# Seven block products for the q, k, z and gate projections, and attention by query block with the output projections as its fill

## The chip, the core and the metric

The kernel runs on one core of a Trainium2 chip. The metric is the device time of one execution in microseconds (us), the median of several runs. Five engines work beside each other, each through its own queue in order: TensorE (PE; matmuls, PEld is its weight load), VectorE (DVE), ScalarE (ACT), GpSimd (POOL) and SyncE (SP), which here only issues DMAs. Matmul results land in PSUM, here in tiles (banks) of up to 128 x 512 floats; the other tiles lie in SBUF. F32R is a rounded float format.

## The reference

One layer on x of 2048 tokens by 1024 channels, all in float32:

- h = RMSNorm(x); one projection of h to 8720 columns: z gate and x, B, C, dt of the SSD branch, q, k, v and z gate of attention, and 2 x 1024 branch gates.
- SSD branch: causal convolution over four tokens, SiLU, softplus of dt, a chunked scan over 16 heads of 64 channels and 128 states; then SiLU gate and group RMSNorm; y_ssd = y @ w_ssd_proj.
- Attention branch, 16 heads of 64 channels: for each query the logits q.k / 8 of the earlier keys; w = sigmoid(logit) times the product of sigmoid(-logit') over all keys between that key and the query; o = w @ v; y_sb = (o * SiLU(z_sb)) @ w_sb_proj.
- merged = sigmoid(gates) weighted sum of y_ssd and y_sb; out = x + RMSNorm(merged @ w_out).

## The kernel before

Tokens are taken in four blocks (tb) of 512. A value that goes into a projection is split into a high and a low F32R part (`split`, lines 680 to 682: a cast on ACT, a subtraction on DVE, both 128 x 512), and each product is three matmuls, high by high, high by low, low by high. A projection tile is 128 output columns by 512 tokens: eight slices of 128 input channels, so 24 matmuls (`product`, `proj`), with the weights split by `prep_w` (line 134) into two halves of 128 x 512.

The work runs in four stages.

1. Input: x is normalized, transposed on PE and kept in SBUF as hh and hl for all four blocks. Then q/k columns 0, 1, 8 and 9 (column 0 also holds dt), 16 tiles in all, and the v columns, which put tokens on partitions (`unit_v`).
2. SSD: per group B and C, then per pair of heads a z and an x column, with convolution on DVE, scan states and outputs in between; the first z column of attention at the end. Results go to `ytd` in DRAM.
3. Attention: 160 steps of (head, query block, key block), head by head; 64 of them on the diagonal. `attn_qk` (lines 827 to 858) makes for each of the four rows i of 128 queries the logits (two matmuls), two sigmoids on ACT, t = sigmoid(-logit) (line 840) and w = sigmoid(logit) (line 842), on the diagonal two masking selects on POOL (844, 846), the running product of t along the keys as a scan on DVE (849), the gating multiply w * t on DVE (850), and a copy of the carry for the next step on POOL (853). `attn_tr` transposes w on PE and ACT copies it to SBUF (870); `attn_av` multiplies with v, and at the end of a head and block o is summed and gated on DVE (890, 891). Between these pieces `fill` hands out projection matmuls at an even rate: the other 34 columns of q, k, z and gates (3264 matmuls) and, in the last head, the y projection of one block (192).
4. Output, block by block: y is normalized (sums of squares by `y_load`, line 693, `y_norm` with the product at 719), y and o are projected, gated, merged, and multiplied by w_out; then the norm and the residual.

The order on PE is the order of the program text, held by `chain`; the other engines are put in order by a scheduler that goes by program order and readiness. `later(n, fn)` issues work n matmuls later. The loop of stage 3:

```
for s in range(len(steps)):
    attn_load(s + 2)
    for i in range(CPB):
        attn_tr(s, i)
        attn_qk(s + 1, i)
        fill(i)
        if i == 1 and s > 0:
            attn_av(s - 1)
            fill(CPB)
```

Of the kernel before, what the change touches and what calls it, by code (L numbers as in the profile page):

```python
# [48 lines left out]
def hybrid_kernel(ctx, tc, x, norm_pre, w_in, b_gate, conv_w, conv_b, dt_bias, a_log, d_skip,  # L49
# [61 lines left out]
    csd = drp.tile([HEADS, L], F32, name="csd")  # L111
    ytd = [drp.tile([D, TB], F32, name=f"ytd{t}") for t in range(NTB)]
# [4 lines left out]
    hp, close_hp = opened(name="hp", bufs=8)  # L117

    def big(dtype, name):
        return hp.tile([P, KT, TB], dtype, name=name, tag="h", bufs=8)  # L120

    hh, hl = [], []
    KH = KT // 2

    def prep_w(pool, bufs, src, col0, eng=None):
        hi, lo = [], []
        for half in range(2):
            raw = pool.tile([P, KH, P], F32, name="wraw", tag="wraw", bufs=2)
            nc.sync.dma_start(
                raw, src[half * KH * P:(half + 1) * KH * P, col0:col0 + P].rearrange("(k p) c -> p k c", p=P))  # L130
            h = pool.tile([P, KH, P], F32R, name="whi", tag="whi", bufs=bufs)
            nc.scalar.copy(h, raw)  # L132
            l = pool.tile([P, KH, P], F32R, name="wlo", tag="wlo", bufs=bufs)
            (eng or nc.vector).tensor_tensor(l, raw, h.bitcast(F32), op=ALU.subtract)  # L134
            hi.append(h)
            lo.append(l)
        return hi, lo
# [23 lines left out]

    def run(gen):
        for _ in gen:
            clock[0] += 1
            while events and events[0][0] <= clock[0]:
                heapq.heappop(events)[2]()
# [53 lines left out]
    ev, close_ev = opened(name="ev", bufs=2)  # L220

    with tc.tile_pool(name="p0", bufs=2) as p0, tc.tile_pool(name="p0p", bufs=1, space=PSUM) as p0p:
        def load_x(tb):
            ts = []
            for c in range(CPB):
                xt = p0.tile([P, D], F32, name="xt", tag="xt", bufs=8)
                nc.sync.dma_start(xt, x[(tb * CPB + c) * P:(tb * CPB + c + 1) * P, :])
                ts.append(xt)
            return ts
# [33 lines left out]
        def normalize(xs, first=False):  # L263
            for c0 in range(0, CPB, 2):
# [7 lines left out]
                if first and c0 == 0:  # L272
                    lead_in.append(i)
# [791 lines left out]
```

## Time and profile before

| | |
|---|---|
| time, median of 3 runs | 3059.14 us (3056.71 to 3060.24) |
| profiled execution: its time, its span | 3057.36 us, 3055.6 us |
| PE busy, instructions | 3012.0 us (99%), 16169 |
| DVE busy | 2140.1 us (70%), 3653 |
| ACT busy | 1585.5 us (52%), 3102 |
| POOL busy | 505.3 us (17%), 1690 |
| granted TensorE clock, mean | 0.995 |
| moved by DMA | 303.84 MB, 99 GB/s |

The span is from the first to the last instruction. Matmuls are pipelined: the busy time of one (0.4 us) is longer than the distance from one to the next, so the pace is read from a long stretch. A busy time counts what an instruction waits for once it has started, also a wait for another engine's access. The chain that ended last is PE for 88%, with the projections alone for 49%.

### The profile page before, as it was taken

The page shows a single profiled execution, that of the slowest core. Times are in us where ns is not written, and L with a number is a line of the kernel's source. Part 1 is how long each engine was busy: PE and PEld are TensorE (multiplying, and loading weights), DVE is VectorE, ACT ScalarE, POOL GpSimd, SP SyncE. Part 2 cuts the span into 40 slices and gives each one's busy share as a digit, 9 for nine tenths or more (in the row PEclk, how much of TensorE's full clock was granted, in tenths as well). Part 3 has the DMA queues.
Part 4 walks back from the last instruction along what each step waited for, and adds up shares of the span by engine and source line. Part 5 has one row for each costly group of instructions (what it writes and reads, how often), then busy time and mean ns, then how long its engine had stood idle before and what let it go on. Part 6 is the DMA issues. An engine that isn't in the chain of part 4 may idle for free.

```text
span 3055.6 us, 47953 instructions
## 1 busy us (share of the span) xinstructions
PE 3012.0 (99%) x16169; PEld 2342.6 (77%) x16169; DVE 2140.1 (70%) x3653; ACT 1585.5 (52%) x3102; POOL 505.3 (17%) x1690
## 2 busy tenths in 40 slices
PE   8999999999999999999999999999999999999998
PEld 6899888788887777777777777777777667888887
DVE  7310578868877777878778878877777798756653
ACT  6221345534546666666666666666666565333321
POOL 0000001001101222222222221222122331101000
PEclk9999999999999999999999999999999999999999
DMA  5522122202233333324323333334233345545452
GB/s 166 142 72 52 28 58 77 78 25 76 81 90 109 101 86 94 93 85 108 94 77 101 97 86 96 89 90 118 66 87 92 114 136 158 178 131 179 131 165 70
DMA packets 298812, 303.84 MB, mean 99 GB/s; under 512 B 55916, under 2 KB 196040, under 8 KB 298568
## 3 DMA queue, kind: packets, MB, share of 16 engines
q1 hardware_dynamic: 298416, 300.73, 34.3%
q8 instruction: 130, 2.13, 0.3%
q14 instruction: 114, 0.93, 0.1%
q10 hardware_dynamic: 152, 0.05, 0.0%
HBM read 208.28 MB, written 92.41 MB: 98 GB/s over the span
## 4 chain that ended last, share of the span: by engine, by line
PE 88%; DVE 7%; DMA 3%; issue 1%; ACT 0%; POOL 0%; SPq 0%; ACTq 0%; DVEq 0%; POOLq 0%
PE proj L74 49%; PE po L74 14%; PE lg L74 8%; PE wtp L77 8%; PE vps L74 6%; DMA csb<-csd 3%; DVE acc L472 1%; PE yp L74 1%; DVE S L538 1%; DVE csb L520 1%; DVE dl L518 1%; DVE dl L514 1%; PE stp L74 0%; DMA xt<-in_x 0%; DVE wlo L134 0%
## 5 line engine op out<-in xcount | busy, mean ns | idle before, releaser
L74 PE MATMUL proj<-hh,whi 128*128 128x512 f32 x1920 | 765.1, 398 | 0.0
L74 PE MATMUL proj<-hl,whi 128*128 128x512 f32 x1920 | 763.0, 397 | 1.1 <-DVE hl L286 0.9
L74 PE MATMUL proj<-hh,wlo 128*128 128x512 f32 x1920 | 763.8, 398 | 0.0
L870 ACT COPY wt<-wtp 128x512 f32<-128x512 f32 (+3 forms) x640 | 336.4, 526 | 396.2 <-PE wtp L77 374.5
L849 DVE TENSOR_TENSOR_SCAN tc<-tc,cy 128x513 f32<-128x513 f32 x384 | 491.7, 1281 | 56.0 <-ACT tc L840 52.3
L850 DVE TENSOR_TENSOR sw<-sw,tc 128x512 f32<-128x512 f32 (+3 forms) x640 | 400.8, 626 | 74.6 <-POOL cy L853 1.4
L74 PEld LDWEIGHTS proj<-hh,whi 128*128 128x128 f32 x1920 | 361.9, 188 | 102.2 <-issue 31.8
L74 PEld LDWEIGHTS proj<-hl,whi 128*128 128x128 f32 x1920 | 361.7, 188 | 102.0 <-issue 31.1
L74 PEld LDWEIGHTS proj<-hh,wlo 128*128 128x128 f32 x1920 | 361.5, 188 | 100.0 <-issue 31.1
L849 DVE TENSOR_TENSOR_SCAN tc<-tc 128x129 f32<-128x129 f32 (+3 forms) x256 | 220.6, 862 | 201.2 <-POOL tc L844 200.3
L840 ACT ACTIVATE tc<-lg 128x512 f32<-128x512 f32 (+3 forms) x640 | 346.3, 541 | 14.5 <-PE lg L74 3.2
L842 ACT ACTIVATE sw<-lg 128x512 f32<-128x512 f32 (+3 forms) x640 | 344.8, 539 | 0.0
L77 PE MATMUL wtp<-ident,sw 128*128 128x128 f32 x2176 | 341.7, 272 | 0.0
L77 PEld LDWEIGHTS wtp<-ident,sw 128*128 128x128 f32 x2176 | 275.5, 140 | 80.1 <-issue 0.3
L74 PE MATMUL lg<-kt,qa 128*128 128x512 f32 (+3 forms) x640 | 284.2, 444 | 2.7 <-ACT sw L842 2.5
L74 PE MATMUL po<-wt,vt 128*64 128x512 f32 (+2 forms) x1280 | 283.5, 554 | 1.7 <-ACT wt L870 1.7
L132 ACT CAST whi<-wraw 128x512 fp32r<-128x512 f32 x248 | 154.4, 623 | 240.9 <-PE proj L74 155.2
L74 PE MATMUL lg<-kt,qb 128*128 128x512 f32 (+3 forms) x640 | 234.3, 366 | 0.0
L134 DVE TENSOR_TENSOR wlo<-wraw,whi 128x512 fp32r<-128x512 f32 x246 | 174.2, 709 | 72.7 <-ACT whi L132 70.1
L74 PEld LDWEIGHTS po<-wt,vt 128*64 128x64 f32 x1280 | 77.9, 136 | 151.9 <-issue 139.1
L504 POOL TENSOR_TENSOR xe<-xd,dec 128x512 f32<-128x512 f32 x32 | 49.8, 1556 | 829.5 <-DVE xd L502 829.5
L839 POOL MEMSET tc<- 128x1 f32 x640 | 62.6, 98 | 739.5 <-DVE sw L850 720.0
(199 smaller groups left out, 4660.1 us busy)
## 6 DMA issues: line engine op xcount, KB each, us to landing
wraw<-in_w_in SPq DMA_DIRECT2D x120, 256.0 KB, 3.0
csb<-csd SPq DMA_DIRECT2D x64, 256.0 KB, 4.3
qa<-qst SPq DMA_DIRECT2D x64, 256.0 KB, 3.7
qb<-qst SPq DMA_DIRECT2D x128, 128.0 KB, 3.8
kt<-kst SPq DMA_DIRECT2D x64, 256.0 KB, 3.3
gtd<-zb SPq DMA_DIRECT2D x64, 256.0 KB, 2.1
wraw<-in_w_ssd_proj SPq DMA_DIRECT2D x64, 256.0 KB, 3.0
scr<-gtd SPq DMA_DIRECT2D x64, 256.0 KB, 3.2
```

The costliest lines, as they stand in the source:

```text
L74: chain(nc.tensor.matmul(*a, **k))
L77: chain(nc.tensor.transpose(*a))
L132: nc.scalar.copy(h, raw)
L134: (eng or nc.vector).tensor_tensor(l, raw, h.bitcast(F32), op=ALU.subtract)
L472: nc.vector.scalar_tensor_tensor(acc, xp[:, i:i + TB], pv[:, col:col + 1], acc, op0=ALU.mult, op1=ALU.add)
L504: nc.gpsimd.tensor_tensor(heads(xe), heads(xd), tok(dec), op=ALU.mult)
L839: nc.gpsimd.memset(t[:, W:W + 1], 1.0)
L840: nc.scalar.activation(t[:, :W], lg[:, :W], AF.Sigmoid, scale=-0.125)
L842: nc.scalar.activation(w[:, :W], lg[:, :W], AF.Sigmoid, scale=0.125)
L849: nc.vector.tensor_tensor_scan(tr, tr, tr, 1.0 if diag else carry[h, qs, i], ALU.mult, ALU.min)
L850: nc.vector.tensor_mul(w[:, :W], w[:, :W], t[:, 1:W + 1])
L870: nc.scalar.copy(wts[s][:, 0:n, i * P:(i + 1) * P], tp[:, 0:n * P].rearrange("p (k q) -> p k q", q=P))
```

## The change

Stage 1 and the projections of q, k, z and gates are written anew.

- 36 columns (14 of q/k, 7 of z, 15 of gates) leave attention's fill and are made ahead of the SSD stage, two columns by two token blocks at a time, for the token pair (0, 1) and then for (2, 3); for (2, 3) the dt column and the second q column make one more pair. Such a unit is a 2 x 2 block product over the two halves of the input channels, done with seven half products of 12 matmuls. Sums of the weight blocks are made on POOL (four per unit, for the unit after), sums of h blocks on POOL and DVE (once per token pair, from a copy of h in DRAM, `hst`); every operand of a product is split again. Banks are read out between products and summed on DVE and ACT, whose order is fixed here by `act` and `dve`.
- h is kept for one pair of blocks at a time and reloaded and split again; v is done in two halves of tokens, with its weights fetched twice.
- Attention runs by query block, last block first, and by head inside it; k and v are loaded for each step. Its fill is the y projections of all blocks (768 matmuls, during the first 65 steps), then for each block done o and out projections (384 each); the last block's output stage follows attention, with 96 matmuls kept back from the one before. The partial y goes to DRAM (`prd`) and comes back.
- In `attn_qk` the gating multiply of rows i = 0 and 1 goes to POOL; tc has four buffers instead of five, sw five instead of six, wtp two instead of three.

The core of the diff:

```diff
+    def sums(p, k):
+        b11, b12, b21, b22 = (piece2() for _ in range(4))
+        for b, t, half in ((b12, 1, 0), (b11, 0, 0), (b22, 1, 1), (b21, 0, 1)):
+            nc.sync.dma_start(b, hst[2 * p + t][:, half * KH + k, :])
+        nc.gpsimd.tensor_tensor(b11, b12, b11, op=ALU.subtract)
+        nc.vector.tensor_tensor(b12, b22, b12, op=ALU.subtract)
+        nc.gpsimd.tensor_tensor(b22, b22, b11, op=ALU.subtract)
+        nc.gpsimd.tensor_tensor(b21, b21, b22, op=ALU.subtract)
+        for n, b in enumerate((b11, b22, b12, b21)):
+            split(b, tops[n][0][:, k, :], tops[n][1][:, k, :])
...
+    ORDER = (1, 5, 6, 2, 7, 4, 3)
+    MOVING = {1: lambda: nat[0, 0], 2: lambda: nat[1, 0], 3: lambda: nat[1, 1], 4: lambda: tops[3],
+              5: lambda: tops[0], 6: lambda: tops[1], 7: lambda: tops[2]}
...
+        def step(self, i):
+            if i == 0:
+                a11, a21, a22, a12 = self.raw
+                s = [ring_w("sum", 4, F32, P) for _ in range(4)]
+                nc.gpsimd.tensor_tensor(s[0], a21, a22, op=ALU.add)
+                nc.gpsimd.tensor_tensor(s[1], s[0], a11, op=ALU.subtract)
+                nc.gpsimd.tensor_tensor(s[2], a11, a21, op=ALU.subtract)
+                nc.gpsimd.tensor_tensor(s[3], a12, s[1], op=ALU.subtract)
+                self.src = {1: a11, 2: a12, 3: s[3], 4: a22, 5: s[0], 6: s[1], 7: s[2]}
+            n = ORDER[i]
+            self.ops[n] = split_w(self.src[n])
...
+    def unit(w, dones, nxt, nxt2, first=False):
+        a = sp1.tile([P, TB], F32, name="qa", tag="sa")
+        c = sp1.tile([P, TB], F32, name="qc", tag="sc")
+        d = sp1.tile([P, TB], F32, name="qd", tag="sd")
...
+        def prod(n, bank, ks, start=False):
+            whi, wlo = w.ops[n]
+            bh, bl = MOVING[n]()
+            for k in ks:
+                for u, m in ((whi, bh), (whi, bl), (wlo, bh)):
+                    matmul(bank, u[:, k, :], m[:, k, :], start=(start and k == ks[0] and m is bh and u is whi),
+                           stop=(k == ks[-1] and u is wlo), skip_group_check=True)
+                    yield
...
+        if first:
+            yield from prod(5, c, al, True)
+        yield from prod(1, a, al, True)
+        p1 = copied()
+        pre(0)
+        if not first:
+            yield from prod(5, c, al, True)
+        yield from prod(6, a, al)
+        u2 = copied()
+        pre(1)
+        yield from prod(2, d, lo2, True)
+        yield from prod(7, a, al)
+        u3 = copied()
+        pre(2)
+        yield from prod(2, d, hi2)
+        dve(nc.vector.tensor_add(u3, u3, c))
+        dve(nc.vector.tensor_add(p1, p1, d))
+        dones[0, 0](p1)
+        pre(3)
+        yield from prod(4, a, al)
+        dones[1, 0](a)
+        pre(4)
+        pre(5)
+        dones[1, 1](u3)
+        pre(6)
+        yield from prod(3, c, al)
+        if nxt2 is not None:
+            nxt2.load()
+        dve(nc.vector.tensor_add(u2, u2, c))
+        dones[0, 1](u2)
...
+    tiles = [("q", i) for i in range(2, 16)] + [("z", j) for j in range(1, 8)] + [("g", j) for j in range(1, 16)]
+    pairs = [(tiles[i], tiles[i + 1]) for i in range(0, len(tiles), 2)]
...
+    def fill_y():
+        units = [(tb, dt) for tb in TBO for dt in range(KT)]
+        w = prep_w(wa, WA, w_ssd, 0)
+        for n, (tb, dt) in enumerate(units):
+            if dt == 0 and n // KT + 1 < NTB:
+                y_prep(n // KT + 1, 12)
+            nw = prep_w(wa, WA, w_ssd, units[n + 1][1] * P) if n + 1 < len(units) else None
+            ps = pp.tile([P, TB], F32, name="proj", tag="pp")
+            yield from product(ps, w, *yops[tb])
+            w = nw
+            gt = pc()
+            nc.sync.dma_start(gt, gtd[tb][dt * P:(dt + 1) * P, :])
+            nc.vector.tensor_mul(gt, gt, ps)
+            nc.sync.dma_start(prd[tb][dt * P:(dt + 1) * P, :], gt)
...
+    def fill_o(tb):
...
+            gt, part = pc(), pc()
+            nc.sync.dma_start(gt, gtd[tb][D + dt * P:D + (dt + 1) * P, :])
+            nc.sync.dma_start(part, prd[tb][dt * P:(dt + 1) * P, :])
+            yield from product(ps, w, oops["h"], oops["l"])
+            w = nw
+            nc.vector.tensor_mul(gt, gt, ps)
+            nc.vector.tensor_add(gt, gt, part)
+            split(gt, mh[:, dt, :], ml[:, dt, :])
+        o_next(tb - 1)
...
-    steps = [(h, qs, kc) for h in range(HEADS) for qs in reversed(range(NTB)) for kc in reversed(range(qs + 1))]
...
+    steps = [(h, qs, kc) for qs in TBO for h in range(HEADS) for kc in reversed(range(qs + 1))]
+    first_step = {qs: min(i for i, s in enumerate(steps) if s[1] == qs) for qs in TBO}
+    LAG = 2
...
+    bounds = [1] + [first_step[qs] + LAG for qs in TBO[1:]] + [len(steps)]
+    sizes = [NTB * KT * 24] + [2 * KT * 24] * (NTB - 1)
+    gens = [fill_y()] + [fill_o(tb) for tb in TBO]
+    for i in range(len(bounds) - 1):
+        plan.append([bounds[i], bounds[i + 1], sizes[i] - (KEEP if i == len(bounds) - 2 else 0)])
...
-        if (h, kc) not in kts:
-            k = ab.tile([P, TB], F32R, name="kt", tag="kt", bufs=4)
+        k = ab.tile([P, TB], F32R, name="kt", tag="kt", bufs=3)
-        t = ab.tile([P, TB + 1], F32, name="tc", tag="tc", bufs=5)
+        t = ab.tile([P, TB + 1], F32, name="tc", tag="tc", bufs=4)
-        w = ab.tile([P, TB], F32, name="sw", tag="sw", bufs=6)
+        w = ab.tile([P, TB], F32, name="sw", tag="sw", bufs=5)
-        nc.vector.tensor_mul(w[:, :W], w[:, :W], t[:, 1:W + 1])
+        (nc.gpsimd if i < 2 else nc.vector).tensor_tensor(w[:, :W], w[:, :W], t[:, 1:W + 1], op=ALU.mult)
-        tp = ap.tile([P, TB], F32, name="wtp", tag="wtp", bufs=3)
+        tp = ap.tile([P, TB], F32, name="wtp", tag="wtp", bufs=2)
```

## Rows read from the trace of the kernel before

**Rows 1.** Stretches by stage: us, busy of each engine, clock, DMA share, GB/s.
```profile
0.00:316.00 316.00, 305.36 (x2128) 283.13 (x2129) 92.31 (x249) 95.40 (x199) 4.57 (x10) 0.99 0.38 106
316.00:931.00 615.00, 604.22 (x3616) 502.25 (x3615) 465.30 (x1148) 273.11 (x388) 52.59 (x48) 1.00 0.24 67
931.00:2556.00 1625.00, 1611.89 (x8221) 1150.23 (x8219) 1286.25 (x1610) 1060.13 (x2226) 406.73 (x1601) 1.00 0.34 95
2556.00:3055.60 499.60, 490.57 (x2209) 406.99 (x2208) 296.28 (x648) 156.86 (x290) 41.37 (x31) 0.99 0.49 150
```

**Rows 2.** Chain in order of time, late: start, us, what.
```profile
2916.03 87.04 PE proj L74 x384
```

**Rows 3.** The attention stretch, projection tiles alone: PE, PEld, DVE, ACT.
```profile
931.00:2556.00 1625.00, 954.07 (x3461) 628.69 (x3459) 57.36 (x84) 88.03 (x137) 1.00 0.34 95
```

**Rows 4.** POOL's selects and adds by line: count, shortest/median/longest ns.
```profile
L846 POOL TENSOR_SCALAR_AFFINE_SELECT sw<-sw x256: 285/293/1316, 926.4 to 2551.1; 128x128 f32<-128x128 f32 x128
L693 POOL TENSOR_TENSOR scr<-scr x21: 1284/1293/2207, 2412.2 to 2875.7; 128x512 f32<-128x512 f32 x21
```

**Rows 5.** Timeline, PE: start, us, operation, idle before and its releaser.
```profile
2429.00 1.27 PE L74 MATMUL sps<-ones,mp 128*128 128x1 f32 x6 [3.89 <-DVE scr L708]
```

**Rows 6.** Groups by line and shape, attention's DVE work: busy us, mean ns.
```profile
L849 DVE TENSOR_TENSOR_SCAN tc<-tc,cy 128x513 f32<-128x513 f32 x384 | 491.7, 1281 | 56.0 <-ACT tc L840 52.3 <-POOL tc L839 2.3
L849 DVE TENSOR_TENSOR_SCAN tc<-tc 128x513 f32<-128x513 f32 x64 | 79.5, 1242 | 30.6 <-POOL tc L844 30.6
L849 DVE TENSOR_TENSOR_SCAN tc<-tc 128x385 f32<-128x385 f32 x64 | 62.0, 969 | 102.8 <-POOL tc L844 102.6
L849 DVE TENSOR_TENSOR_SCAN tc<-tc 128x257 f32<-128x257 f32 x64 | 48.2, 753 | 31.4 <-POOL tc L844 31.4
L849 DVE TENSOR_TENSOR_SCAN tc<-tc 128x129 f32<-128x129 f32 x64 | 30.9, 483 | 36.4 <-POOL tc L844 35.7 <-POOL tc L839 0.7
L850 DVE TENSOR_TENSOR sw<-sw,tc 128x512 f32<-128x512 f32 x448 | 316.5, 707 | 52.9
L850 DVE TENSOR_TENSOR sw<-sw,tc 128x384 f32<-128x384 f32 x64 | 36.4, 568 | 8.3 <-POOL cy L853 0.9
L850 DVE TENSOR_TENSOR sw<-sw,tc 128x256 f32<-128x256 f32 x64 | 28.4, 443 | 6.6
L850 DVE TENSOR_TENSOR sw<-sw,tc 128x128 f32<-128x128 f32 x64 | 19.5, 305 | 6.8 <-POOL cy L853 0.5
L891 DVE TENSOR_TENSOR o<-o,zl 64x512 f32<-64x512 f32 x64 | 43.9, 686 | 2.4 <-DMA zl<-zsd 0.4
```

**Rows 7.** Timeline, DVE and POOL, where POOL's instruction starts first.
```profile
2412.21 1.28 POOL L693 TENSOR_TENSOR scr<-scr 128x512 f32<-128x512 f32 x1 [1.08 <-ACT scr L691]
2412.30 1.74 DVE L850 TENSOR_TENSOR sw<-sw,tc 128x512 f32<-128x512 f32 x1
```

**Rows 8.** Timeline, DVE and POOL, where a DVE scan starts first.
```profile
2452.25 1.28 DVE L849 TENSOR_TENSOR_SCAN tc<-tc,cy 128x513 f32<-128x513 f32 x1
2452.41 2.20 POOL L682 TENSOR_TENSOR yl<-mp,yh 128x512 fp32r<-128x512 f32 x1
2453.45 0.72 DVE L719 SCALAR_TENSOR_TENSOR mp<-mp,pv,rb 128x512 f32<-128x512 f32 x1
2454.09 1.06 DVE L850 TENSOR_TENSOR sw<-sw,tc 128x512 f32<-128x512 f32 x1
```

**Rows 9.** Timeline, DVE alone, one instruction behind the other.
```profile
2511.22 0.69 DVE L850 TENSOR_TENSOR sw<-sw,tc 128x512 f32<-128x512 f32 x1
2511.83 1.28 DVE L849 TENSOR_TENSOR_SCAN tc<-tc,cy 128x513 f32<-128x513 f32 x1
```

**Rows 10.** Three short stretches, columns as in the first group.
```profile
2430.00:2432.00 2.00, 2.00 (x10) 1.82 (x10) 1.27 (x13) 0.00 (x0) 0.00 (x0) 0.50 0.01 4
2443.78:2461.66 17.88, 13.04 (x54) 8.27 (x53) 16.85 (x17) 11.79 (x24) 16.15 (x19) 0.81 0.33 99
2500.00:2556.00 56.00, 51.63 (x264) 35.44 (x262) 49.60 (x65) 36.10 (x78) 15.48 (x43) 1.00 0.31 90
```

More of the change, by code (lines that the diff above doesn't have):

```diff
@@ L285, in turn @@
+    def turn(tb, xs, k, direct):
+        ps = sp1.tile([P, TB], F32, name="xtp", tag="x", bufs=2)
+        for c in range(CPB):
+            transpose(ps[:, c * P:(c + 1) * P], xs[c][:, k * P:(k + 1) * P], ident)
+        g = pv[:, ROW_NP + k:ROW_NP + k + 1]
+        if direct:
             nc.scalar.mul(hh[tb][:, k, :], ps, g)
@@ new lines, in hybrid_kernel @@
+    for _ in range(WARM):
+        matmul(warm[:, :P], ones, ones, start=True, stop=True)
+    nat_slots(0)
+    junk = slot(TS + 7, F32, "junk").rearrange("p k c -> p (k c)")
+    normalize(xs[0], junk, True)
+    w0 = prep_n(COL_DT, nc.gpsimd)
+    pvp = pp.tile([P, TB], F32, name="pvp", tag="pp")
+    transpose(pvp[:, :NROW], pvr, ident[:NROW, :NROW])
+    after(nc.vector.tensor_copy(pv, pvp[:, :NROW]), lead_in[0])
+    xs.append(load_x(0, 1))
+    dsk_r = scn.tile([P, HEADS], F32, name="dsk_r")
@@ new lines, in hybrid_kernel @@
+    w1 = prep_n(COL_DT + P)
+    normalize(xs[1], junk)
+    for k in range(KT):
+        later(16 + 4 * k, lambda k=k: turn(1, xs[1], k, True))
+    run(lead)
+    run(proj(w1, 0, done_qk(1, 0)))
+    wv = prep_v(0)
+    run(proj(w0, 1, done_dt(1)))
+    run(proj(w1, 1, done_qk(1, 1)))
+    later(4, sum_slots)
+    for k in range(KH):
+        later(5 + 40 * k, lambda k=k: sums(0, k))
+    W = [Weights(col(p), col(q)) for p, q in pairs]
+    later(96, W[0].load)
+    for i in range(4):
+        later(100 + 20 * i, lambda i=i: W[0].step(i))
@@ new lines, in hybrid_kernel, with chain_pairs @@
+    for c in range(2 * CPB):
+        run(unit_v(0, c, wv))
+    flush()
+    for i in range(4, 7):
+        W[0].step(i)
+    def chain_pairs(p, work, first):
+        work[1][1].load()
+        fixed["on"] = True
+        for i, ((m1, m2), w) in enumerate(work):
+            dones = {(0, 0): target(m1, 2 * p), (0, 1): target(m1, 2 * p + 1),
+                     (1, 0): target(m2, 2 * p), (1, 1): target(m2, 2 * p + 1)}
+            run(unit(w, dones, *(work[i + n][1] if i + n < len(work) else None for n in (1, 2)), first and i == 0))
+        free_order()
@@ L692, in square @@
             if k:
                 nc.gpsimd.tensor_tensor(s0, s0, s1, op=ALU.add)
[L694 to L713 removed]
+            box["s", g] = [s1, s0]
@@ new lines, in sums @@
+        def sums(g):
+            acc = box["s", g][1]
+            sps = pp.tile([P, TB], F32, name="sps", tag="pp")
+            for c in range(CPB):
+                matmul(sps[:, c:c + 1], acc[:, c * P:(c + 1) * P], ones[:, 0:1], start=True, stop=True)
+            v, r, t = (ab.tile([P, CPB], F32, name=n, tag=n, bufs=1) for n in ("yv", "yr", "yt"))
+            nc.vector.tensor_scalar(v, sps[:, :CPB], 1.0 / 512, EPS, op0=ALU.mult, op1=ALU.add)
+            with tc.high_priority():
+                newton_rsqrt(v, r, t)
+            box["r", g] = r
```

1038 lines of the change are left out of this document (539 added, 499 removed).

## The prediction

> **What bounds the kernel now.** I read the share of TensorE over the whole span first, and then cut the span at the four stages, because an average over stages with different limits says little. The reader is to see in the stage table [rows 1] that TensorE is busy in all of them: 305 of 316 us in the first (input norm, four q/k columns, the v columns), 604 of 615 in the SSD stage, 1612 of 1625 in attention, 491 of 500 in the output stage. So TensorE's issue is the bound everywhere, and VectorE (DVE) comes next with 1286 us in the attention stage. The pace is read from a stretch of 384 matmuls that nothing interrupts: 87.04 / 384 = 0.2267 us each [rows 2], 5.44 us for a tile of 24. In attention, 3461 matmuls are projections used as fill [rows 3]: 3461 x 0.2267 = 785 us. The other 840 of the 1625 us are attention's own scores, transposes and value products: 160 steps, 64 on the diagonal and 96 full ones.
>
> **The change on TensorE.** A unit of the seven-product scheme does four tiles with 7 x 12 = 84 matmuls instead of 96. The pairs are 18 for the first two token blocks and 19 for the last two (the dt and q1 columns join there): 37 units, 37 x 12 = 444 matmuls, 444 x 0.2267 = 101 us less. That is all that leaves TensorE. The rest moves, stage by stage:
> - First stage. Before, it holds 16 plain tiles. Now 4 plain tiles stay, so 12 x 24 x 0.2267 = 65 us go, and 37 x 84 x 0.2267 = 705 us come: 316 - 65 + 705 = 956 us. The weight sums and splits of a unit cost GpSimd (POOL) 4 x 1.29 [rows 4] and DVE 7 x 0.69 plus seven evictions, some 10 us, beside 19 us of matmuls; ScalarE (ACT) has about as much. They are for the unit after, so TensorE hides them. A bank is read back while 6 or 12 other matmuls run (1.4 or 2.7 us), against one copy. I cost them at nothing; the cover is gone where DVE is late on one bank, and each 0.5 us of that in every unit is 18 us.
> - Joins. Six places start with fresh operands (reload of h for the second pair, first unit, v columns twice, weights after pools are closed, first y tile). I take one wait of the size of TensorE's 3.89 us [rows 5] at each, 23 us; bounds 0 and 60 (a gain is excluded, for nothing that stalls now is taken away there).
> - SSD stage, with the first z and gate column: unchanged, 615 us.
> - After attention: one output block is left, 384 matmuls, and 96 that were kept back: 480 x 0.2267 = 109 us, and the 9 us that this stage now sits idle [rows 1]: 118 us, where 500 stood.
> - DMAs: k and v are fetched at each step, 96 times 384 KB more, all on SP's queue, two steps ahead of use, with the DMA engines busy 0.34 in that stage [rows 1]. Nothing, unless steps fall under 4 us.
>
> **The change in attention** decides. The fill shrinks from 3461 matmuls to 1824 (y 768, three output blocks 1056): TensorE needs 840 + 1824 x 0.2267 = 1254 us. DVE and ACT keep all of attention's work, so they are late next. DVE's scans are 491.7 + 79.5 + 62.0 + 48.2 + 30.9 = 712 us, the gating multiplies 316.5 + 36.4 + 28.4 + 19.5 = 401, o's two steps 2 x 43.9 = 88 [rows 6]. The change gives the multiplies of query rows i = 0 and 1 to POOL: 2 x 96 x 0.707 + 28.4 + 19.5 = 184 us leave DVE. The fill brings to it some 252 splits, sums and products with both inputs in SBUF and 100 that read PSUM, at 0.69, and the splits' casts to ACT, which loses as many evictions (it is busy 1060 of the 1625 us now [rows 1]). DVE: 712 + 217 + 88 + 243 + 30 for small ones = 1290 us, already over TensorE's 1254.
>
> But DVE and POOL don't run side by side. In [rows 7] a POOL add of 1.28 us starts first, and the DVE multiply behind it takes 1.74 us instead of 0.69: it ends 0.55 after the add. In [rows 8] it is the other way round: the POOL subtract waits for the scan, takes 2.20 us and ends 1.08 after it; the DVE product that reads PSUM passes meanwhile in 0.72, while the multiply of two SBUF tiles waits, and ends 0.54 after POOL. The select of POOL, 0.29 alone, has a maximum of 1.32 [rows 4]. So POOL's tensor work and those DVE instructions that read two SBUF tiles take turns, and their times add up. A multiply that moves to POOL frees 0.61 us of turn (a DVE multiply and the next scan are 0.61 apart [rows 9]) and takes 1.07 to 1.29.
>
> The GPSIMD Engine Reference of the Trainium skill says in its section 8 that POOL shares its SBUF interfaces with DVE and contends with DVE instructions that have two SBUF inputs; it doesn't say that they exclude each other, which only the rows show. Its section 4.1 keeps elementwise work on DVE, because two-input operations take POOL about twice as long (1.28 against 0.69 here, so the trace agrees); by that factor a moved multiply would be an estimated 1.38 us and the stage 192 x 0.2 = 38 us longer than below.
>
> The turns of a full step: four scans 4 x 1.28, two DVE multiplies 2 x 0.61, two POOL multiplies 2 x 1.07 to 1.29: 8.5 to 8.9 us. Of a diagonal step: scans 0.48 + 0.75 + 0.97 + 1.24 [rows 6], DVE multiplies 0.49 + 0.61 (0.08 under their rows, by which neighbours overlap), eight selects at 0.2 to 0.29, POOL multiplies of 128 and 256 columns, not in the trace, bounded at 0.8 to 1.0 together by the share of columns of the 512 wide one: 7.0 to 7.9. Together 96 x 8.7 + 64 x 7.5 = 1315 us. The fill's two-SBUF work: 64 weight splits for y, 48 for the output, 16 of w_out, 24 and 32 splits of y and o, 24 merged splits and 24 sums, 20 residual sums, 64 gatings of o: 316 x 0.61 to 0.70 = 193 to 221 us; 18 sums of squares on POOL, 19 to 23. I take 228. The sum is 1543 us, with ends 1476 and 1604, at full use of the turns.
>
> Is full use real? Where eight POOL subtracts of y fell into attention, a stretch of 17.88 us holds DVE busy 16.85 and POOL busy 16.15 [rows 10], each counted with its waiting: 4 scans, 4 multiplies, 2 splits and 8 POOL subtracts come to about 17.3 us of turns, 97%. In that stretch TensorE was busy 13.04. So I take 1543 / 0.965 = 1600 us for the stage. TensorE is then used 78% there, and the stage is hardly shorter than now, though its fill has halved.
>
> **The sum**, on the profiled execution (3057.4 us, span 3055.6; the median of the runs is 1.8 above it, which I leave): 956 + 23 + 615 + 1600 + 118 + 2 = **3313 us**, 8% slower. Low end 956 + 615 + 1476 + 118 + 2 = 3167; high end with joins 60, a stage of 1604 / 0.945 = 1700 and 20 for latencies in the output block 956 + 60 + 615 + 1700 + 138 + 2 = 3471. Within 0.2%, some 6 us, a measurement of this kernel can't tell a change from none.
>
> **Rivals.**
> - The other side: DVE and POOL overlap after all. The place is attention, the price 1600 - 1330 = 270 us, and it decides when more than 95% of POOL's multiply time lies beside DVE's. Then DVE's 1290 us are the bound, at 97% 1330, and the sum is 956 + 23 + 615 + 1330 + 118 + 2 = 3044, or 3003 with no waits at all: faster. For it: DVE does finish PSUM reads beside POOL [rows 8]. Against it: every overlap that I looked at is a turn. 10%, of which 8 faster and 2 about equal or just slower.
> - Worse than turns: a chain. POOL works in order, so a multiply that waits for its turn holds the select and the carry copy behind it, for which the next scans wait; scan, POOL multiply, copy and next scan then stand in a row. A full step is 4 x 1.28 + 2 x (1.29 + 0.5) + 2 x 0.71 = 10.1 us plus fill, a diagonal one 8.3: 970 + 531 + 316 x 0.7 = 1720 us plus POOL's small pieces and DVE's PSUM reads, 1810: 3524 us. For it: the DVE scan waits for selects now already. Against it: four t tiles let memsets run ahead. 12%.
> - The clock falls. After TensorE's wait of 3.89 us [rows 5] the granted clock is 0.50 of full speed, the lower level of 1.2 GHz [rows 10]. If half of attention's TensorE work ran there at twice the time, the 1254 us would be 1254 + 627 = 1881, over DVE and POOL: 3595 us. The page TensorE: Matmul & The Clock Gate of the Trainium skill, part 1, has the clock halve after idling and come back with activity, and the rows agree. Against it: in the last 56 us of attention TensorE is busy 51.63, with waits spread over every step, at a clock of 1.00 [rows 10], and the waits forecast here are 2 us in a step, in four or five pieces. 4%.
>
> **How the numbers follow.** Turns 74%, 3167 to 3471, the likeliest at 3313; overlap 10%, chain 12%, clock 4%. The range from 3140 to 3490 leaves out the overlap and most of the last two. Faster 0.08, same 0.02, slower 0.90.
>
> **What would show it.** Steps right: units at 0.227 us a matmul and TensorE over 97% busy until the SSD stage; that stage unchanged; in attention POOL's multiply at a median over 1.5 us and DVE's two-SBUF multiplies stretched past 0.69, TensorE about 80% busy, clock 1.00, the stage near 1600; some 118 us after it. Wrong: POOL's multiplies at 1.3 us while DVE keeps 0.69, and a stage near 1330; or TensorE waiting inside the units, which would mean that the seven products pay for their banks.

## The result and the profile after

The changed kernel takes 3312.28 us (median of 4 runs, 3310.98 to 3314.28) against 3059.4 for the kernel before: ratio 1.0829, 95% interval 1.081 to 1.0848. The forecast was 3313 us, but two of its terms are off by some 55 us each, in opposite directions. The profile is of an execution of 3310.98 us. The stretches by stage of the kernel after answer to [rows 1] (columns as there; the borders are the first SSD projection at 1028, the first logits at 1645, the last value product at 3190.5):

```profile
0.00:1028.00 1028.00, 971.17 (x4941) 814.54 (x4941) 497.77 (x759) 420.92 (x766) 254.43 (x182) 0.98 0.49 144
1028.00:1645.00 617.00, 605.68 (x3600) 500.44 (x3601) 464.63 (x1154) 272.83 (x389) 58.17 (x43) 0.99 0.26 73
1645.00:3190.50 1545.50, 1347.64 (x6704) 874.52 (x6703) 1337.54 (x1660) 1043.32 (x2267) 862.91 (x1933) 0.96 0.46 129
3190.50:3309.30 118.80, 110.08 (x484) 89.97 (x480) 57.21 (x156) 21.68 (x46) 0.00 (x0) 0.98 0.40 125
```

In the SSD stage TensorE is nearly full (606 of 617 us). In the first it is idle for 57 us (971 of 1028). In attention it is busy 1348 of 1545, and DVE about as long, 1338. Attention needs 1545 us although its fill was halved.

Attention's groups on POOL and DVE by shape (busy us, mean ns, idle before) answer to [rows 6]:

```profile
L1184 POOL TENSOR_TENSOR sw<-sw,tc 128x512 f32<-128x512 f32 x192 | 306.0, 1594 | 142.5 <-DVE tc L1183 51.5 <-PE lg L74 23.7 <-ACT sw L1176 20.6
L1187 POOL COPY cy<-tc 128x1 f32<-128x1 f32 x384 | 180.8, 471 | 149.0 <-DVE tc L1183 140.5 <-DVE yt L103 5.6 <-DVE yt L104 1.6
L1183 DVE TENSOR_TENSOR_SCAN tc<-tc,cy 128x513 f32<-128x513 f32 x384 | 519.9, 1372 | 33.3 <-ACT tc L1174 30.4 <-POOL tc L1173 1.0 <-POOL sw L1184 0.9
L1184 DVE TENSOR_TENSOR sw<-sw,tc 128x512 f32<-128x512 f32 x256 | 193.3, 756 | 21.7 <-DVE yv L958 0.3
L703 DVE TENSOR_TENSOR wlo<-wraw,whi 128x512 fp32r<-128x512 f32 x115 | 105.6, 918 | 1.1 <-ACT whi L701 0.6 <-ACT wt L1206 0.2
```

The scan's mean went from 1281 to 1372 ns, the mean of DVE's 512 wide multiply from 707 to 756 [rows 6]: both now hold time in which they wait for POOL. Most single multiplies do not; over all shapes (shortest/median/longest ns) the medians are 1304 on POOL and 692 on DVE:

```profile
L1184 POOL TENSOR_TENSOR sw<-sw,tc x320: 408/1304/2464, 1647.4 to 3179.0; 128x512 f32<-128x512 f32 x96, 128x128 f32<-128x128 f32 x64
L1184 DVE TENSOR_TENSOR sw<-sw,tc x320: 542/692/1579, 1656.3 to 3185.1; 128x512 f32<-128x512 f32 x96, 128x384 f32<-128x384 f32 x64
```

A short timeline of the two engines (start, us, operation, idle before) shows how, and answers to [rows 7, 8]; the first block is POOL's, the second DVE's:

```profile
2000.16 1.89 POOL L1184 TENSOR_TENSOR sw<-sw,tc 128x512 f32<-128x512 f32 x1 [1.15 <-DVE tc L1183]
2002.00 0.64 POOL L1187 COPY cy<-tc 128x1 f32<-128x1 f32 x1
2002.82 1.10 POOL L1184 TENSOR_TENSOR sw<-sw,tc 128x512 f32<-128x512 f32 x1
...
1999.91 1.26 DVE L1183 TENSOR_TENSOR_SCAN tc<-tc,cy 128x513 f32<-128x513 f32 x1
2001.09 1.52 DVE L703 TENSOR_TENSOR wlo<-wraw,whi 128x512 fp32r<-128x512 f32 x1
2002.63 0.69 DVE L1226 TENSOR_TENSOR o<-o,po 64x512 f32<-64x512 f32 x1
2003.36 1.11 DVE L1227 TENSOR_TENSOR o<-o,zl 64x512 f32<-64x512 f32 x1
```

POOL's multiply starts at 2000.16 beside a scan, and ends at 2002.05, 0.88 after the scan's end (2001.17). The subtraction behind the scan ends 0.56 after POOL. The sum that reads PSUM (L1226) passes beside POOL's next multiply in 0.69, the two-SBUF multiply behind it waits until POOL is done (1.11). These are the turns of the prediction. But a POOL multiply takes 0.88 to 1.10 of a turn here, and part of it lies beside DVE's PSUM reads.

What TensorE waited for in attention (total us, times, longest), and DVE's longest wait, for POOL's mask on the diagonal:

```profile
PE wtp L77 <- POOL sw L1184: 97.7, 100, 2.1
PE wtp L77 <- ACT wt L1206: 31.1, 18, 4.9
PE lg L74 <- ACT sw L1176: 23.4, 39, 4.8
PE wtp L77 <- DVE sw L1184: 11.0, 12, 2.1
DVE tc L1183 <- POOL tc L1178: 121.5, 147, 4.4
```

And in the stage with the units, from 80 to 1030 us:

```profile
PE qc L74 <- DVE pc L420: 17.1, 9, 2.7
PE qa L74 <- ACT vt L485: 8.8, 1, 8.8
PE qc L74 <- ACT vt L485: 6.6, 2, 5.1
PE vps L74 <- ACT vt L485: 4.9, 4, 2.5
```

### The profile page after: what moved, and what is told of

Its sections match the earlier page's. It is cut to its first block, busy times and chain, and to the rows that moved or that the text cites. A ratio compares the mean times of both kernels' runs of the same rounds, so it can differ in the third digit from the quotient of the medians.

```text
span 3309.3 us, 48770 instructions
## 1 busy us (share of the span) xinstructions
PE 3034.6 (92%) x15725; PEld 2279.5 (69%) x15725; DVE 2357.1 (71%) x3727; ACT 1758.8 (53%) x3466; POOL 1175.5 (36%) x2158
## 5 line engine op out<-in xcount | busy, mean ns | idle before, releaser
L1183 DVE TENSOR_TENSOR_SCAN tc<-tc,cy 128x513 f32<-128x513 f32 x384 | 519.9, 1372 | 33.3 <-ACT tc L1174 30.4
L77 PE MATMUL wtp<-ident,sw 128*128 128x128 f32 x2176 | 360.9, 282 | 147.0 <-POOL sw L1184 97.7
L1184 POOL TENSOR_TENSOR sw<-sw,tc 128x512 f32<-128x512 f32 (+1 forms) x320 | 387.4, 1210 | 209.3 <-DVE tc L1183 111.7
L157 DVE TENSOR_TENSOR wlo<-sum,whi 128x512 fp32r<-128x512 f32 x148 | 127.5, 862 | 258.3 <-ACT whi L156 258.2
L1183 DVE TENSOR_TENSOR_SCAN tc<-tc 128x129 f32<-128x129 f32 (+3 forms) x256 | 220.1, 861 | 123.5 <-POOL tc L1178 121.5
L74 PE MATMUL proj<-nh,whi 128*128 128x512 f32 x736 | 293.1, 398 | 4.4 <-ACT whi L701 3.7
L74 PE MATMUL proj<-nh,wlo 128*128 128x512 f32 x736 | 293.3, 399 | 0.0
L74 PE MATMUL proj<-nl,whi 128*128 128x512 f32 x736 | 292.3, 397 | 0.6 <-DVE nl L313 0.6
L1184 DVE TENSOR_TENSOR sw<-sw,tc 128x512 f32<-128x512 f32 (+1 forms) x320 | 229.1, 717 | 29.0 <-POOL sw L1180 0.7
L1187 POOL COPY cy<-tc 128x1 f32<-128x1 f32 x384 | 180.8, 471 | 149.0 <-DVE tc L1183 140.5
L703 DVE TENSOR_TENSOR wlo<-wraw,whi 128x512 fp32r<-128x512 f32 x172 | 145.6, 846 | 60.4 <-ACT whi L701 59.9
L390 ACT COPY pc<-qa 128x512 f32<-128x512 f32 x111 | 64.8, 584 | 224.8 <-PE qa L74 224.5
L157 DVE TENSOR_TENSOR wlo<-raw,whi 128x512 fp32r<-128x512 f32 (+1 forms) x145 | 110.3, 763 | 99.0 <-ACT whi L156 97.5
```

The costliest lines, as they stand in the source:

```text
L74: chain(nc.tensor.matmul(*a, **k))
L77: chain(nc.tensor.transpose(*a))
L157: i = (eng or nc.vector).tensor_tensor(l, src, h.bitcast(F32), op=ALU.subtract)
L390: act(nc.scalar.copy(t, a))
L1183: nc.vector.tensor_tensor_scan(tr, tr, tr, 1.0 if diag else carry[h, qs, i], ALU.mult, ALU.min)
L1184: (nc.gpsimd if i < 2 else nc.vector).tensor_tensor(w[:, :W], w[:, :W], t[:, 1:W + 1], op=ALU.mult)
```

## The experiments

The theory: attention is paced by DVE's own two-input work and by POOL's turns with it, no longer by TensorE. Rivals: POOL runs beside DVE after all; TensorE sets the pace through its own waits; a chain of latencies from logits to scan to transpose sets it. Lengths of attention below are from the first logits to the last value product. e2 to e5 are one execution each, e1 and e6 to e8 two.

**Who does the multiplies.** Three versions of line 1184, and one of the kernel before.

```diff
 # e1
-        (nc.gpsimd if i < 2 else nc.vector).tensor_tensor(w[:, :W], w[:, :W], t[:, 1:W + 1], op=ALU.mult)
+        nc.vector.tensor_tensor(w[:, :W], w[:, :W], t[:, 1:W + 1], op=ALU.mult)
 # e2
+        nc.gpsimd.tensor_tensor(w[:, :W], w[:, :W], t[:, 1:W + 1], op=ALU.mult)
 # e3
+        if i >= 2:
+            nc.vector.tensor_tensor(w[:, :W], w[:, :W], t[:, 1:W + 1], op=ALU.mult)
 # e4, on the kernel before, line 850
-        nc.vector.tensor_mul(w[:, :W], w[:, :W], t[:, 1:W + 1])
+        (nc.gpsimd if i < 2 else nc.vector).tensor_tensor(w[:, :W], w[:, :W], t[:, 1:W + 1], op=ALU.mult)
```

> The changed kernel with all gating multiplies back on DVE. Turns (DVE instructions with two SBUF inputs and POOL's tensor work exclude each other): 320 POOL multiplies, some 284 us of turns, are replaced by 154 us on DVE, the attention stage falls from 1543 to about 1470 and the time from 3312 to 3235..3260. Rival, no turns (POOL works beside DVE, and attention is bound by DVE's own instructions, or by the smaller buffers and the new order of steps): DVE gets 184 us more, and the time rises to 3410..3470.

> The changed kernel with the gating multiplies of all four rows on POOL. Turns: 320 more multiplies at 1.1 instead of 0.6 us, +175 us of turns, time about 3490. Rival, no turns: DVE loses 229 us of work, POOL has time left, and the time falls to 3100..3200.

> The changed kernel with the gating multiply of query rows i = 0 and 1 left out (w is used as it is). Turns: 284 us of turns go, attention is then bound by DVE's 1290 us or TensorE's 1254, stage near 1330, time about 3100. Rival, no turns: POOL was beside the bound, the stage stays, time 3290..3312.

> The kernel before with only this edit: the gating multiplies of rows 0 and 1 on POOL. Turns: its attention stage needs some 1260 us of turns now and 1390 then, of 1625 that TensorE sets, so it is covered: 3055..3080. Rival, a chain (POOL in order holds selects and carry copies behind the multiply): DVE and TensorE wait in every step, 3120 or more. Rival, no turns: 3055..3060.

Measured: e1 3282.21 (ratio to before 1.0726, 1.0692 to 1.076), e2 3423.51, e3 3155.36, e4 3064.5 beside 3058.67 of the kernel before. Attention in e1, e2 and e3, one row of each:

```profile
1644.00:3164.00 1520.00, 1339.88 (x6704) 867.98 (x6702) 1388.01 (x1979) 1040.56 (x2267) 507.87 (x1613) 0.97 0.47 131
```
```profile
1645.70:3303.60 1657.90, 1379.05 (x6703) 884.62 (x6702) 1238.71 (x1339) 1049.06 (x2267) 1278.85 (x2253) 0.95 0.44 120
```
```profile
1646.00:3035.40 1389.40, 1304.27 (x6704) 871.68 (x6703) 1224.72 (x1659) 1032.05 (x2267) 491.44 (x1613) 0.98 0.52 144
```

e1 to e3 each go the way of the turns, none by the size I gave. The 320 multiplies of rows 0 and 1 cost 1545 - 1389 = 156 us on POOL, 1520 - 1389 = 131 us on DVE. So their move to POOL costs 25 us, where the prediction's prices make it some 130 (POOL 256 to 312, DVE about 155); the other 320, moved too, cost 1658 - 1545 = 113. e3 also speaks against the overlap rival: by that rival POOL's multiplies are free, and leaving them out would change nothing. DVE runs the same instructions in both (1660 and 1659), and is busy 1338 us with POOL's multiplies beside it and 1225 without: 113 of the 156 us are time that DVE's own instructions spent waiting for POOL (the scan's mean is 1372 ns in one and 1286 in the other). The other 43 are idle time of DVE. What part of them comes from the turns isn't shown, because e3 also takes a dependency away: the transposes of rows 0 and 1 no longer wait for scan and multiply (97.7 us of TensorE's waits were for POOL's multiply). In e4 attention takes 1633 us beside 1631 (TensorE busy 1611 of the 1625 of [rows 1]): the same move costs nothing that shows where TensorE is the bound. That rules out the chain in the kernel before; turns and overlap forecast nearly the same there.

**Is TensorE the bound in attention?**

```diff
+        if thin:   # in attention
+            for k in range(KT):
+                matmul(ps, hi[k // KH][:, k % KH, :], sh[:, k, :], start=(k == 0), stop=(k == KT - 1))
...
```

> Leaves out two of the three matmuls of every k step in the projections that attention uses as fill (1216 of 1824 in the stage, 320 of 480 behind it); everything that DVE, POOL, ACT and the queues do stays. TensorE then needs 1254 - 276 = 978 us in the attention stage. Theory (the stage is paced by DVE and by POOL's turns with it): the stage stays within 40 us of 1543, only the part behind attention shrinks by 73 us; total 3200 to 3240. Rival (TensorE sets the pace in attention, its waits are small): the stage falls to about 1270, total 2950 to 3000.

Measured: 3292.61. Attention:

```profile
1647.40:3181.70 1534.30, 1219.07 (x5808) 740.52 (x5806) 1329.02 (x1659) 1038.90 (x2267) 924.08 (x1933) 0.90 0.47 130
```

The edit thins less than the expectation says. It changes `product`, which makes the y and o projections; the output projections (tile outp, 480 matmuls in the stage in both kernels) have a loop of their own and stay whole. The projection tiles of the stage, in the changed kernel and in e5:

```profile
1645.00:3190.50 1545.50, 441.23 (x1369) 255.53 (x1367) 38.46 (x57) 1.29 (x2) 0.96 0.46 129
1647.40:3181.70 1534.30, 205.44 (x472) 97.31 (x471) 38.45 (x57) 1.29 (x2) 0.90 0.47 130
```

So 897 matmuls are gone, 203 us at 0.2267, not 1216 and 276. The stage is 11 us shorter; DVE's busy time is nearly as before (1329), and the granted clock falls from 0.96 to 0.90. If TensorE set the pace, the stage would have lost most of the 203 us: it doesn't. The total missed its 3200 to 3240. Behind attention 128 matmuls are gone, 29 us instead of the 73 forecast, and that part is 10 us shorter: TensorE now waits there for a bank's read-out (7.2 us) and for weights (5.7 us), at a clock of 0.90.

**Do the seven products pay?**

```diff
...
-            n = ORDER[i]
-            self.ops[n] = split_w(self.src[n])
+            n = ((0, 0), (0, 1), (1, 0), (1, 1))[i]   # column, half: four plain blocks
+            self.ops[n] = split_w((a11, a12, a21, a22)[i])
...
+        for x, ((m, t), bank) in enumerate((((0, 0), a), ((0, 1), c), ((1, 0), d), ((1, 1), a))):
+            for n in range(2):
+                yield from half(m, t, bank, n)
...
```

> The 37 units compute their four tiles as plain projections, 96 matmuls instead of the 84 of the seven products, in the same place, without weight sums and without bank read-backs. 444 more matmuls at 0.2267 us are 101 us. Theory (the seven products save what they promise, less the 25 to 40 us that TensorE was seen waiting on late sums): 3312 + 60 to 80, plus up to 15 us for a join that starts less prepared, 3370 to 3410. Rival (bank read-backs and sums eat the saving): 3340 or less.

Measured: 3434.88 (ratio 1.1224, 1.1191 to 1.1256), 122.6 us over the changed kernel, above what was expected. The SSD stage starts at 1150.3 instead of 1028.1, attention has the same 1545. 101 us are the 444 matmuls. Of the other 21, the waits from 80 to 1150 us show some 14 (48.2 us ahead of the tiles in bank a, where the units waited 34.9 in all):

```profile
PE qa L74 <- DVE hlt L247: 21.0, 15, 1.4
PE qa L74 <- ACT pc L262: 11.9, 14, 1.1
PE qa L74 <- DVE pc L255: 8.5, 6, 1.4
```

This plain order uses one bank twice in a unit and waits for its read-out; that is the experiment's own cost. The edit also loads h for the second pair of blocks in another order. The rest isn't traced.

**Why the first stage is too long.**

```diff
         pre(5)
+        if nxt2 is not None:
+            nxt2.load()
         dones[1, 1](u3)
         pre(6)
         yield from prod(3, c, al)
-        if nxt2 is not None:
-            nxt2.load()
```

> The weight loads of the unit after next are issued one product earlier, ahead of the last two tiles' writes on SP's queue. Theory (the q units lose 2.7 us in every second unit because the weights of the next unit land late and POOL's sums of them run into DVE's work): the q units of both pairs lose less, 15 to 35 us off, 3278 to 3297. Rival (the loss is the read-back of the banks itself): 3305 to 3315.

Measured: 3291.98 (ratio 1.0757, 1.0725 to 1.0788), 20 us less; the SSD stage starts at 1005.4. One stretch of 20 us among the q units, after and in e7:

```profile
140.00:160.00 20.00, 17.29 (x72) 13.72 (x71) 13.72 (x15) 8.27 (x15) 10.60 (x7) 0.96 0.62 175
```
```profile
140.00:160.00 20.00, 20.00 (x88) 16.27 (x87) 9.55 (x14) 7.87 (x15) 6.36 (x5) 1.00 0.58 168
```

TensorE's wait for the bank sum L420 fell from 17.1 us to 1.6:

```profile
PE qc L74 <- DVE pc L420: 1.6, 3, 0.7
```

So 23 us of the stage were lost to late weights: the edit changes nothing but the place of their loads, which stood on SP's queue behind the tiles' writes. That POOL's sums of them then came late and took turns with DVE just when a bank had to be read fits the two rows (POOL busy 10.60 and 6.36, DVE 13.72 and 9.55), but no run shows it alone.

**Taking the multiplies away.** sigmoid(l) = 1 - sigmoid(-l), so a weight is the difference of two neighbours of the scan: w(j) = t(j+1) - t(j). Summed by parts, the output is the sum of t(j) times (v(j-1) - v(j)), plus the last value row of each block of 128 queries. The scan itself is then transposed.

```diff
-        w = ab.tile([P, TB], F32, name="sw", tag="sw", bufs=5)
-        nc.scalar.activation(w[:, :W], lg[:, :W], AF.Sigmoid, scale=0.125)
-        (nc.gpsimd if i < 2 else nc.vector).tensor_tensor(w[:, :W], w[:, :W], t[:, 1:W + 1], op=ALU.mult)
...
+            nc.vector.tensor_tensor(vts[s], vps.pop(s), vts[s], op=ALU.subtract)   # once a step
...
+        nc.sync.dma_start(vp[1:P], vst[h // 4][0:P - 1, h % 4, kc * CPB:(kc + 1) * CPB, :])
+        nc.sync.dma_start(vp[0:1, lo:], vst[h // 4][P - 1:P, h % 4, kc * CPB + lo - 1:(kc + 1) * CPB - 1, :])
```

> Attention's gated sum is rewritten by parts: a weight is the difference of two neighbours of the scan, so the value product takes the scan itself against differences of neighbouring value rows, plus one value row per block of 128 queries. That takes away all 640 gating multiplies, 640 of ACT's 1280 sigmoids and half of POOL's selects, and adds one 256 column subtract on DVE in each of 160 steps and some 0.3 us per head and query block. DVE's own work falls from 1384 (all multiplies on DVE) to about 1060 us, POOL's turns to selects and copies, below TensorE's 1254. Theory (DVE and its turns with POOL pace the stage): the stage falls to TensorE's bound, 1290 to 1390, total 3060 to 3160. Rival (a latency chain from scores to scan to transpose paces it, whatever DVE's load): the stage stays over 1450, total over 3220.

> The sum by parts again, with DVE no longer waiting for a transfer at the head of its queue: keys and both value blocks are fetched three steps ahead instead of two (5 value and 4 shifted value buffers), the subtract stands late in the step before the value product, and POOL's memset is gone from the loads. The early weight loads of stage 1 are in too (they took 20 us off alone). Theory (attention is paced by DVE's two input work and its turns with POOL; the run before failed only on late value blocks): attention falls to TensorE's bound, 1270 to 1350, total 1005 + 620 + 1270 to 1350 + 119 = 3015 to 3095. Rival (a latency chain from scores to scan to transpose paces the stage): attention stays over 1450, total over 3195.

> As the run before it, and in stage 1 a sixth buffer for raw weights, so that the loads of the unit after next are issued two products earlier still, ahead of all four tiles' writes. Theory (what the q units still lose is late weights): 5 to 20 us less than the run before it. Rival (what is left in stage 1 is joins and the start): within 4 us of it.

Measured: e8 3529.57 (ratio 1.1533, 1.15 to 1.1567), e9 3480.72 (1.1366, 1.1349 to 1.1383), e10 3489.58 (1.1398, 1.1379 to 1.1417). All three missed; attention takes 1744 and 1712 us in e8 and e9. What they show is a wait of DVE for loads that I had added to. DVE's longest waits in e8's attention, and then in e9's:

```profile
DVE vt L1219 <- DMA vt<-vst: 315.5, 79, 11.9
```
```profile
DVE vt L1235 <- DMA vt<-vst: 288.2, 85, 11.8
```

Loading one step further ahead (e9) took only 27 us off this wait. The subtraction needs vt, the value block that was loaded before, and vp, the shifted one that is new. In the stretch below it stands behind a wait each time (e9; start, us, idle before):

```profile
2003.13 0.43 DVE L1235 TENSOR_TENSOR vt<-vp,vt 128x256 f32<-128x256 f32 x1 [6.36 <-DMA vt<-vst]
2012.16 0.43 DVE L1235 TENSOR_TENSOR vt<-vp,vt 128x256 f32<-128x256 f32 x1 [2.69 <-DMA vt<-vst]
2020.74 0.43 DVE L1235 TENSOR_TENSOR vt<-vp,vt 128x256 f32<-128x256 f32 x1 [2.83 <-DMA vt<-vst]
2030.14 0.42 DVE L1235 TENSOR_TENSOR vt<-vp,vt 128x256 f32<-128x256 f32 x1 [4.21 <-DMA vt<-vst]
```

The wait is put down to vt, whose shape is as before. What is new on SP's queue is vp, which the profile page of e9 lists with 127.0 KB, one row short of 128, and a transfer of one row behind it, which takes SP itself a median of 1.62 us and up to 7.19 to issue:

```profile
vp<-vst SPq DMA_DIRECT2D x160, 127.0 KB
L1186 SPq DMA_DIRECT2D vp<-vst x160: 280/1623/7190, 1606.5 to 3316.7; - x160
```

In the trace's packets of e9 from 1900 to 2300 us, exactly one 1 KB packet is under way for 195 of the 400 us; at 46 ns each, 127 of them one after the other are 5.8 us. The Trainium skill (DMA: Bandwidth & Descriptors, section "Why a DMA increments its semaphore by 16 and not by 1") has the rule: a transfer is spread over as many of the 16 engines as divide its slowest dimension, so that 127 partitions go to one engine. The trace agrees. Why the wait is put down to vt these rows don't show; that vp's loads are the cause is for the next run to show. e10's sixth weight buffer did not shorten stage 1, it ended 8 us later (1012.8 against 1004.7); I didn't find why.

**The same with 128 rows.** The store of v gets one row more, the last row of the chunk before. Against e9:

```diff
-    vst = [drp.tile([P, 4, NCH, HD], F32, name=f"vst{i}") for i in range(HEADS // 4)]
+    vst = [drp.tile([P + 1, 4, NCH, HD], F32, name=f"vst{i}") for i in range(HEADS // 4)]
...
-        nc.sync.dma_start(vp[1:P], vst[h // 4][0:P - 1, h % 4, kc * CPB:(kc + 1) * CPB, :])
+        nc.sync.dma_start(vp, vst[h // 4][0:P, h % 4, kc * CPB:(kc + 1) * CPB, :])
...
```

> The sum by parts with the early weight loads, and the value rows shifted by one are now read by a transfer of 128 rows, since the store of v keeps one row more (the last row of each chunk ahead of the next); in the run before it 127 rows were read, and their 1 KB packets went one at a time, 127 x 46 ns = 5.8 us a step beside which everything else on that path waited. Theory (attention is paced by DVE and its turns with POOL; both runs by parts were held by that transfer): attention falls to TensorE's bound, 1270 to 1350, total 3015 to 3095. Rival (a latency chain from scores to scan to transpose paces the stage): attention stays over 1450, total over 3195.

Measured: 3079.98 (ratio 1.0068, 1.0051 to 1.0085). e9 and e11 from 1900 to 2300, e11's attention, and what is left of DVE's wait:

```profile
1900.00:2300.00 400.00, 331.94 (x1660) 227.66 (x1659) 267.87 (x391) 197.48 (x378) 90.33 (x167) 0.91 0.42 123
```
```profile
1900.00:2300.00 400.00, 392.16 (x2069) 265.38 (x2069) 326.93 (x446) 247.69 (x484) 124.21 (x212) 0.99 0.56 162
1639.30:2958.30 1319.00, 1272.61 (x6704) 866.00 (x6702) 1095.87 (x1682) 793.55 (x1627) 404.08 (x721) 0.99 0.58 165
DVE vt L1237 <- DMA vt<-vst: 32.6, 23, 3.0
```

One 1 KB packet alone is under way for 14 of these 400 us now, and vp lands in 3.1 us (median on the profile page). e11 also drops the one row transfer; the two aren't told apart by a run. Attention falls to 1319 us with TensorE busy 1273: it is the bound again, as the theory had it, once DVE's work is down from 1338 to 1096 and the scan's mean back at 1280 ns. The latency chain as forecast, over 1450 whatever DVE's load, is out. But e11 takes away more than the multiplies: one sigmoid per row from ACT (busy 1043 before, 794 now), a select per diagonal row and the memsets from POOL (863, 404), and tc has six buffers instead of four. What each is worth no run shows.

**The best version.** e11's trace names what TensorE still waited for: the new value rows (9.4 us at the start of attention, at a clock of 0.74), ACT's copies of the last v tiles, and the transposes' banks.

```diff
+        later(50, turned)                                  # value rows turned later
...
-        ps = sp1.tile([P, TB], F32, name="vps", tag=("sa", "sc", "sd")[c % 3])
+        ps = sp1.tile([P, TB], F32, name="vps", tag=(("sc", "sd", "sa") if i == 0 else ("sa", "sd", "sc"))[c % 3])
...
-        nc.gpsimd.tensor_tensor(b11, b12, b11, op=ALU.subtract)      # and two more sums of h
+        nc.vector.tensor_tensor(b11, b12, b11, op=ALU.subtract)
...
-        tp = ap.tile([P, TB], F32, name="wtp", tag="wtp", bufs=2)
+        tp = ap.tile([P, TB], F32, name="wtp", tag="wtp", bufs=3)
```

> The run before it with four waits of TensorE taken out that its trace names: the one value row per block is turned 50 matmuls after its load instead of right behind it (9.4 us waited at the start of attention, and the clock fell to 0.74 there), the last v tiles before the units lie in the banks that the units need last (6.4, 4.9 and 2.5 us waited on ACT's copies), the operand sums of the token blocks go from POOL to DVE (their turns kept ACT's copies late at the same places), and a third bank for the transposes (17.8 us waited). If TensorE is the bound again in every stage, each of these waits comes off the time: 3080 - 9 - 10 - 10 to 18 = 3040 to 3055, just under the kernel before. Rival (the waits move to the next late engine, as earlier gains in attention did): 3065 to 3080.

Measured: 3048.2 (median of 7; 3045.8 to 3056.45) against 3058.51: ratio 0.997, 0.9958 to 0.9982. It is clearly faster than the changed kernel, and 10 us, 0.3%, under the one before: the interval leaves 1 out, but single executions of the two overlap (up to 3056.45 and from 3054.58), so the two are about equal. Its stages (the profiled execution took 3055.4):

```profile
0.00:995.70 995.70, 966.42 (x4942) 813.09 (x4942) 471.38 (x785) 422.53 (x766) 213.66 (x158) 0.99 0.50 149
995.70:1616.90 621.20, 609.47 (x3609) 503.81 (x3610) 467.06 (x1161) 273.40 (x389) 58.33 (x39) 0.99 0.26 74
1616.90:2935.80 1318.90, 1268.64 (x6704) 865.42 (x6702) 1095.69 (x1682) 793.96 (x1627) 403.76 (x721) 0.99 0.57 166
2935.80:3053.70 117.90, 109.79 (x484) 90.06 (x480) 58.15 (x159) 21.48 (x46) 0.00 (x0) 0.99 0.39 126
```

The gain over e11 lies ahead of attention, which starts at 1616.9 instead of 1639.3; the third bank gave nothing (1319 in both). TensorE's wait for the banks went, and one for the sigmoids of the logits grew from 6.3 us to 26.4: there the wait moved on, as the rival had it, though the total is the theory's (e11, then e12):

```profile
PE wtp L77 <- ACT wt L1233: 17.8, 16, 2.8
PE lg L74 <- ACT tc L1206: 26.4, 22, 3.1
```

The sum by parts was not tried on the kernel before, where DVE isn't the bound.

## Why the prediction came out

- **Sign and mechanism: right.** "TensorE is then used 78% there, and the stage is hardly shorter than now": it is used 87% (1348 of 1545), and the stage is 80 us shorter than the 1625 of [rows 1]. e5 shows that TensorE doesn't set its pace, e3 that POOL's multiplies hold DVE up by 113 us, e11 that TensorE is the bound again once DVE has 240 us less and ACT and POOL are relieved too.
- **Attention, 1600 forecast, 1545 measured.** The step that failed is the division by 0.965 ("So I take 1543 / 0.965"), and under it the turns' prices. The sum of 1543 is met by chance. By the same prices e3 would have turns of about 1260, and takes 1389; e2 some 1720, and takes 1658. POOL's multiplies were priced at their full turn (256 to 312 us for 320), and cost 156. Full use of the turns is what fails: without POOL's multiplies neither TensorE (1304 of 1389) nor DVE (1225) is full, so there are gaps into which part of a POOL multiply can fall. What the sum left out is waits from engine to engine: in the changed kernel DVE is idle for 208 us of attention, 121.5 of them ahead of scans that wait for POOL's mask, so a part of the chain that the prediction gave 12% is in the stage beside the turns.
- **First stage, 956 and four joins of 3.9 forecast, so 972; 1028 measured.** "I cost them at nothing; the cover is gone where DVE is late on one bank": the place was named, the size was not. Late weights cost 23 us (e7). The joins were sized by one wait of 3.89 [rows 5]; single ones took 8.8 and 5.1 us, and behind the last v tiles they come to 20.3, where four of 3.9 are 15.6. e12's edits, made at two of them, bring the stage from 1009 (e11) to 996. The other 28 of the 56 us are not broken down.
- **The saving of the seven products: right,** 101 forecast, 122 by e6, of which some 14 are that experiment's own waits.
- **SSD stage and the end:** 617 against 615, 118.8 against 118.
- **The signs named for it** were in part the wrong ones. POOL's multiply was to have a median over 1.5 us and DVE's to stretch past 0.69. The 512 wide ones have means of 1.59 and 0.76, but over all shapes the medians are 1.30 and 0.69, which the prediction had named as a sign against itself, together with a stage near 1330. The stage (1545) and e3 decide, not the medians; it is more the scan (1281 to 1372 ns) than the multiply that waits. TensorE was to be over 97% busy until the SSD stage, and is 94% (971 of 1028). The clock was to stay at 1.00 and is 0.96 in attention: the clock rival has a small part.
- **Rivals.** The overlap would need 1330, and e3 has 1389 with no multiply on POOL at all; the chain's 1810 is reached by none of the kernels, not even by e8 and e9 with their late transfers. One rival stands untested: the change also took a buffer each from tc, sw and wtp, and no run gives them back to it alone (e12's third transpose bank gained nothing, but there the multiplies are gone). POOL's memset of a tc buffer waits 242 us for the DVE multiply that frees it; but in the kernel before, with five, it waited 719 us while TensorE was full (1612 of 1625).
- **Two sums** of the prediction are off by an addition, without weight for it: its terms give 3314, and the overlap "with no waits at all" (3003) still holds the joins; without them it is 2981.

So the total fits because attention is 55 us under and the first stage 56 over. The range of 3140 to 3490 would have covered either error alone; that the point came within 1 us is luck.

## What to carry to other kernels

When work leaves the engine that is the bound in a stage, add up what the next engine needs there before counting a gain: halving TensorE's fill gained 80 us of 370, and most of the rest came only when DVE's, POOL's and ACT's work went too. Price an engine's contention by taking its instructions away in an experiment, not by the longest waits of a timeline, and compare the other engine's busy time over the same instructions. Count what an experiment's edit really removed, in its trace, before reading its time. A transfer that is new on a path is to be looked at by its shape, not by its bytes.

## What the runs showed of the hardware

- POOL and DVE hold each other up: with 320 multiplies on POOL beside them, the same DVE instructions of attention are busy 1338 us instead of 1225 (e3).
- A copy of 128 x 1 on POOL (the carry) has a mean of 471 ns in the kernel after; one in the timeline above took 0.64 us beside a DVE subtraction, and others 0.18. Small POOL work waits for turns as well.
- With loads of 127 rows, and of one row behind each, a single 1 KB packet was under way alone for 195 of 400 us (e9), with loads of 128 rows for 14 (e11). TensorE did 1660 and 2069 matmuls in these 400 us, and attention took 1712 and 1319 us.
- The granted clock, 1.00 in attention before [rows 1], is 0.96 there after, 0.90 in e5, and 0.99 in e11, which has as many matmuls as the kernel after but fewer waits between them. In e5 203 us of matmuls went and TensorE's busy time fell by 129 (1348 to 1219): part of what a lighter TensorE stage gains is given back.
